# The beginning of a transformer block in two halves of the tokens: where column reads, the last transpose copies and the squares of the second half stand

## The chip, the cores and the metric

The kernel runs on one core of a Trainium2 chip. The metric is the device time of one launch in microseconds (us); lower is better. A core has TensorE (PE, with its weight loads PEld), VectorE (DVE), ScalarE (ACT), GpSimd (POOL), and SyncE (SP), which here issues most loads. Each engine works off its own instructions in the order in which they are written; between engines, an instruction waits for semaphores.

## What is computed

One layer of a diffusion transformer on 1024 latent tokens and 256 context tokens of width 1024. The parts that matter here come first in it:

```python
mod_x = (silu(c) @ w_mod + b_mod); mod_c = silu(c_ctx) @ w_mod + b_mod
sh1, sc1, ... = split(mod_x, 6);   csh1, csc1, ... = split(mod_c, 6)
h_x = rmsnorm(x,   g_pre_mix) * (1 + sc1)  + sh1
h_c = rmsnorm(ctx, g_pre_mix) * (1 + csc1) + csh1
u, q, k, v = split(h @ w_in)     # u: first 512 columns of w_in
```

Behind that stand a pooling mixer on u, neighbourhood attention with the context's keys, an output projection, and a squared-ReLU MLP, each with its norm and gate.

## The kernel before

The change touches the first 45 us alone. There the kernel normalises the latent tokens, turns them by 128 x 128 transposes on TensorE so that the width lies on the partitions, scales and shifts them with the modulation, and multiplies them with the first 512 columns of `w_in`.

**Tiles.** The tokens are eight tiles `x0` to `x7` of 128 rows. Tiles 0 to 3 are the first half (b = 0), tiles 4 to 7 the second (b = 1). The width is eight chunks k of 128. `xT[k]` holds chunk k of all tokens, turned. Each float32 operand is split in a high part (`fp32r`) and a low part (the rest), and a product is three passes: high x high, low weight x high operand, high weight x low operand. `wu0`, `wu1` ... are the weights for chunks 0 and 1, 2 and 3, ...; `wu0h` and `wu0l` are their parts; `hx0_1` is the operand of half 0 and chunk 1; `pu0_0` is the sum of output group 0 and half 0.

**The steps of a half.** `squared(n)` sums the squares of tile n on ScalarE (L154, 1024 columns, into `ms_x`). `rooted(n)` adds epsilon on VectorE (L159, `vt_x`) and raises to the power -1/2 on POOL (L163, `rt_x`). `normalised(n)` scales the tile on VectorE (L386). `turned` transposes one block on TensorE (L368) into a PSUM bank: `pxt0` to `pxt7` for the first half, one chunk each, and `pxb0` to `pxb2` for the second half, chunks 0 and 1, 2 and 3, 4 and 5. `put` and `kept_two` copy from there to `xT` (L373), on ScalarE or VectorE.

**The modulation.** For chunks 0 to 3, `chunk_sums(k, kh)` is 16 small matmuls (L402) of the modulation's weights with silu(c) and silu(c_ctx), in two halves kh of the inner width; a page of weights is loaded for each. `chunk_row` copies the row to SBUF (L406, `mrow`), `picked` turns it to columns on TensorE (L416), and `chunk_scale(k, pt, v)` makes scale `a1` (L431) and shift `s1` (L432) of chunk k on VectorE: v = 0 for the latent tokens, v = 1 for the context. The context's columns are used only much later, by `context`. `latent_high` makes the high part of an operand (L447 on ScalarE, L449 on VectorE), `latent_low` the low part (L453, then L454 on VectorE), `half_weight` the parts of half a weight page.

**Banks.** PSUM has six banks in the pool `ps1` and two lasting ones in `ps_t`. A name decides which:

```python
if name[:2] == "pm" or name in ("pxt5", "pxb2", "pxb3", "pxb4", "pct2", "pct3"):
    return lasting(name)                       # ps_t, 2 buffers
return ps1.tile([P, 512], F32, tag="mm", name=name)
```

So the lasting ones are taken in the order `pxt5`, `pm0_0` (chunk 0), `pm0_1` (chunk 1), `pxb2`, `pm1_0` (chunk 2), `pm1_1` (chunk 3), `pxb3` and so on. Each new tile takes over a buffer whose readers are done, and the first instruction that writes it waits for them. `picked` writes its columns into the same bank as the sums of its chunk, so that a bank of a chunk is read last by `chunk_scale`.

**What sets the order.** In this part the order on each engine is the order of the calls in the program: `in_order` keeps TensorE, ScalarE, VectorE, SyncE and POOL to it. All loads are issued by SyncE in the order: tiles 0 to 3, modulation pages and weights of chunks 0 and 1, tiles 4 to 7, pages and weights of chunks 2 and 3, pages of quarter 2, `wu2`, pages of quarter 3, `wu3`, the context.

Of the kernel before, what the change touches and what calls it, by code (L numbers as in the profile page):

```python
# [22 lines left out]
NT = SEQ // P  # L23
# [80 lines left out]
def hybrid_block(ctx, tc, x, ctx_in, w_mod, mod_pages, b_mod, gp1, gp2, w_in, pool_w, rpb, w_out, w1, w2, vectors,  # L104
# [14 lines left out]
    def sm(name, n, bufs=1):  # L119
        return small.tile([P, n], F32, tag=name.split("_")[0], name=name, bufs=bufs)  # L120

    def page(name, dt=F32):
        return act.tile([P, 1024], dt, tag="pg", name=name)
# [29 lines left out]
    def mean_square(junk, src, ms):  # L153
        nc.scalar.activation(junk, src, AF.Square, scale=D ** -0.5, accum_out=ms)  # L154

    def rsqrt_of(name, ms, more=None):
        v = sm(f"v{name}", 1, 4)
        if more is None:
            nc.vector.tensor_scalar_add(v, ms, EPS)  # L159
        else:  # L160
            nc.vector.scalar_tensor_tensor(v, ms, EPS, more, add, add)  # L161
        r = sm(f"r{name}", 1, 4)
        nc.gpsimd.tensor_tensor(r, v, nhalf, ALU.pow)  # L163
        return r
# [129 lines left out]
    with tc.tile_pool(name="ps1", bufs=6, space=PSUM) as ps1, tc.tile_pool(name="tmp1", bufs=3) as tmp:  # L294
# [75 lines left out]
        def put(copy, src, k, n):  # L370
            if xT[k] is None:
                xT[k] = page(f"xT{k}")
            copy(xT[k][:, n * P : n * P + src.shape[-1]], src)  # L373

        on_act, on_dve = nc.scalar.copy, nc.vector.tensor_copy
        means = {}

        def squared(n):
            means[n] = sm(f"ms_x{n}", 1, 4)
            mean_square(page(f"jkx{n}"), xn[n], means[n])  # L380

        def rooted(n):
            means[n] = rsqrt_of(f"t_x{n}", means[n])

        def normalised(n):
            nc.vector.tensor_scalar_mul(xn[n], xn[n], means[n])  # L386
# [28 lines left out]
        def picked(pt, mr, j):  # L415
            nc.tensor.matmul(pt[:, 4 * j : 4 * j + 4], mr[:, j * P : (j + 1) * P], pck, start=True, stop=True)  # L416
# [12 lines left out]
        def chunk_scale(k, pt, v):  # L429
            ks = slice(k, k + 1)  # L430
            nc.vector.scalar_tensor_tensor(a1[v][:, ks], pt[:, 2 + v : 3 + v], b_sc[:, ks], g1c[:, ks], add, mul)  # L431
            nc.vector.tensor_tensor(s1[v][:, ks], pt[:, v : v + 1], b_sh[:, ks], add)  # L432
# [10 lines left out]
        def latent_high(b, k, copy):  # L443
            h = hx[b][k] = page(f"hx{b}_{k}", F32R)
            src, scale, shift = xT[k][:, b * 512 : (b + 1) * 512], a1[0][:, k : k + 1], s1[0][:, k : k + 1]
            if copy is on_act:
                nc.scalar.activation(h[:, :512], src, AF.Identity, bias=shift, scale=scale)  # L447
            else:
                nc.vector.tensor_scalar(h[:, :512], src, scale, shift, mul, add)  # L449

        def latent_low(b, k):
            h, src = hx[b][k], xT[k][:, b * 512 : (b + 1) * 512]
            nc.vector.tensor_scalar(src, src, a1[0][:, k : k + 1], s1[0][:, k : k + 1], mul, add)  # L453
            nc.vector.tensor_tensor(h[:, 512:], src, h[:, :512].bitcast(F32), sub)  # L454
# [7 lines left out]
        def passes(b, js, k, n):  # L462
            if not pus[b]:
                pus[b] += [bank(f"pu{j}_{b}") for j in js]
            low, r = ((0, hx[b][k][:, :512]), (1, hx[b][k][:, :512]), (0, hx[b][k][:, 512:]))[n]
            for j in js:
                nc.tensor.matmul(pus[b][j], wk(wgt, k, low, j * P, P), r,  # L467
                                 start=(k == 0 and n == 0), stop=(k == KT - 1 and n == 2))

        def some_sums(b, js, k):  # L470
            for n in range(3):
                passes(b, js, k, n)
# [14 lines left out]
        def half_weight(q, i, part):  # L487
            cs = slice(i * 512, (i + 1) * 512)
            hi, lo = (t[:, cs] for t in wgt[q])
            part(raw_u[q][:, cs], hi, lo) if part is low_part else part(raw_u[q][:, cs], hi)  # L490

        pxt = [bank(f"pxt{k}") for k in range(5)] + [bank("pxt5"), bank("pxt6"), None]
        whole, pt = {}, {}

        def chunk_sums(k, kh):
            if kh == 0:
                whole[k] = bank(f"pm{k // 2}_{k % 2}")
            mod_sums(k // 2, whole[k], kh, k % 2)

        def chunk_row(k):  # L500
            pt[k] = whole[k][:, 384:388]
            return mod_kept(f"{k // 2}_{k % 2}", whole[k], P)

        def first_turned(n, ks):
            for k in ks:
                turned(pxt[k][:, n * P : (n + 1) * P], n, k)
# [21 lines left out]
        first_turned(3, range(4, KT - 1))  # L528
        put(on_act, pxt[0], 0, 0)
        half_weight(0, 0, lambda src, hi: nc.gpsimd.tensor_copy(hi, src))  # L530
        chunk_scale(0, pt[0], 0)
        put(on_dve, pxt[1], 1, 0)
        latent_high(0, 0, on_act)
        half_weight(0, 0, low_part)
# [3 lines left out]
        put(on_act, pxt[5], 5, 0)  # L538
        put(on_dve, pxt[4], 4, 0)
        put(on_dve, pxt[6], 6, 0)  # L540
        chunk_scale(0, pt[0], 1)
        chunk_sums(1, 0)
        passes(0, range(4), 0, 0)
        chunk_sums(1, 1)
# [3 lines left out]
        picked(pt[1], mr, 0)  # L548
        chunk_scale(1, pt[1], 0)
        latent_high(0, 1, on_dve)  # L550
        half_weight(0, 1, low_part)
        latent_low(0, 1)
        passes(0, range(4), 0, 2)
        pxt[7] = bank("pxt7")
        for n in range(4):
            first_turned(n, (7,))
        squared(4)
        put(on_act, pxt[7], 7, 0)
        for n in range(5, NT):
            squared(n)  # L560
        some_sums(0, range(4), 1)

        pxb = [bank(f"pxb{i}") for i in range(3)]
# [6 lines left out]
        def kept_two(copy, ks, n):  # L570
            for k in ks:
                put(copy, two(k), k, n)
# [4 lines left out]
                turned(ps[:, (n - 4) * P : (n - 3) * P], n, k)  # L577
            put(on_act, ps, k, 4)

        rooted(4)  # L580
        chunk_scale(1, pt[1], 1)
        rooted(5)
        normalised(4)
        rooted(6)
        normalised(5)
        rooted(7)
# [14 lines left out]
        kept_two(on_act, (2,), 6)  # L601
        mr = chunk_row(2)
        latent_high(1, 1, on_act)
        half_weight(1, 0, high_part)
        some_sums(1, range(2), 0)
        picked(pt[2], mr, 0)
        chunk_scale(2, pt[2], 0)
        latent_low(1, 1)
        latent_high(0, 2, on_act)
        half_weight(1, 0, low_part)  # L610
        latent_low(0, 2)
        kept_two(on_act, (4,), 6)
        kept_two(on_dve, (5,), 6)
        chunk_scale(2, pt[2], 1)
        for kh in range(2):
            chunk_sums(3, kh)
        mr = chunk_row(3)
# [858 lines left out]
    with tc.tile_pool(name="ps2", bufs=6, space=PSUM) as ps2:  # L1476
# [6 lines left out]
      with ExitStack() as tmp2:  # L1483
# [21 lines left out]
        def out_bank_sums(name, a, w):  # L1505
            ps = [bank(f"{name}_{t}") for t in range(4)]
            for t in range(4):
                out_sums(ps[t], a, w, t, True)
            return ps
# [32 lines left out]
        with tc.issue_after(projected[ET.DVE]), tc.issue_after(projected[ET.Activation]), in_order(ET.Activation, ET.DVE) as added:  # L1542
# [20 lines left out]
            v = out_bank_sums("pov", "S3", wt3)  # L1563
# [220 lines left out]
        def part(name):  # L1784
            return tmp.tile([P, 512], F32, tag="z", name=name, bufs=7)
# [263 lines left out]
        with tc.issue_after(first[ET.PE]), in_order(ET.PE, ET.Activation, ET.DVE, ET.SP):  # L2049
# [5 lines left out]
            def four(name):  # L2055
                return [bank(f"{name}_{t}") for t in range(4)]
# [78 lines left out]
            v, z = four("pyv"), four("pyz")  # L2135
# [68 lines left out]
```

## Time and profile before

| what | value |
|---|---|
| median of 3 runs | 1034.26 us (1032.35 to 1034.46) |
| profiled execution: time | 1033.65 us |
| profiled execution: span of the instructions | 1031.9 us |
| mean granted TensorE clock | 0.996 of full |
| TensorE busy, whole span | 1014.0 us (98%) |
| TensorE busy, 0 to 45 us | 35.66 us, granted clock 0.92 |
| TensorE busy, 45 to 200 us | 155.00 us, granted clock 1.00 |
| VectorE and ScalarE busy, 0 to 45 us | 22.59 and 23.47 us |
| DMA in the first 45 us | 373 GB/s, 97% of the 16 engines' time |

Times in the profile are counted from the first instruction. A row of the timeline gives start, duration, engine, line of the kernel, operation, what it writes and reads (without buffer numbers), a count where rows were merged, and in brackets how long the engine was idle before it and what ended that. An engine's name with a q is its sequencer, which issues DMAs. "issue" means that the profile shows nothing that the engine waited for. The granted clock is TensorE's clock as a share of full speed.

### The profile page before, as it was taken

The numbers are of one execution on the slowest core, as the hardware profiler recorded it, in microseconds if no ns is written. First come the engines' busy times: TensorE is split into PE (matmuls) and PEld (weight loads), VectorE is DVE, ScalarE is ACT, GpSimd is POOL, SyncE is SP. The second block draws the span as 40 slices with busy tenths as digits, with TensorE's granted clock in tenths as the row PEclk, the third lists the DMA queues.
The fourth block names the chain that finished last, engine by engine and source line by source line (L and its number), as shares of the span: only waits on it lengthen the run. The fifth ranks groups of instructions, "written<-read, shape, count | busy, mean of one in ns | idle before, by whom it ended". The sixth has DMA issues, their size and how long they took to land.

```text
span 1031.9 us, 16144 instructions
## 1 busy us (share of the span) xinstructions
PE 1014.0 (98%) x5962; PEld 839.8 (81%) x5962; DVE 747.8 (72%) x1164; ACT 544.2 (53%) x949; POOL 149.3 (14%) x231
## 2 busy tenths in 40 slices
PE   7899999999999999999999999999999999999997
PEld 6678888887898888888888888888888888888886
DVE  5578947877786687878998888855766666547576
ACT  5475155337888546776555544555543334334441
POOL 2011020047775312310000000000000000000002
PEclk9999999999999999999999999999999999999999
DMA  9769698814337965794786666636967766546555
GB/s 361 297 181 368 198 292 287 286 26 124 74 74 203 217 193 189 244 260 164 248 277 203 221 200 218 214 113 238 325 222 281 241 228 224 199 168 199 171 182 224
DMA packets 117023, 222.72 MB, mean 216 GB/s; under 512 B 9488, under 2 KB 46992, under 8 KB 116944
## 3 DMA queue, kind: packets, MB, share of 16 engines
q1 hardware_dynamic: 90448, 171.14, 49.2%
q0 software_dynamic: 9360, 19.58, 9.4%
q10 hardware_dynamic: 17136, 30.97, 8.0%
q8 instruction: 47, 0.77, 0.3%
q14 instruction: 32, 0.26, 0.1%
HBM read 168.16 MB, written 52.45 MB: 214 GB/s over the span
## 4 chain that ended last, share of the span: by engine, by line
PE 95%; POOL 1%; ACT 1%; issue 1%; DVE 1%; DMA 0%; POOLq 0%; DVEq 0%; ACTq 0%
PE pu L467 4%; PE pa L1247 3%; PE phz L221 3%; PE phv L221 3%; PE phx L221 3%; PE pyx L221 3%; PE phx L223 3%; PE phz L223 3%; PE phv L223 3%; PE pyx L222 3%; PE pyx L223 3%; PE pyv L222 3%; PE pyv L221 3%; PE pyz L222 3%; PE pyz L221 3%; PE phx L222 3%
## 5 line engine op out<-in xcount | busy, mean ns | idle before, releaser
L1193 ACT ACTIVATE sp<-sp,nm 128x640 f32<-128x640 f32 (+1 forms) x64 | 51.5, 804 | 9.6 <-DVE ri L1197 4.9
L1182 DVE CUSTOM_DVE_ANT_0 sp<-S,tab 128x640 f32<-128x640 f32 (+1 forms) x56 | 44.5, 795 | 14.1 <-PE pz L1213 9.6
L1789 ACT ACTIVATE c<-c 128x512 f32<-128x512 f32 x48 | 30.3, 631 | 46.0 <-DVE c L1909 26.6
L169 ACT CAST wpS<-S 128x512 fp32r<-128x512 f32 x64 | 38.8, 616 | 28.1 <-DVE S L1762 11.3
L221 PE MATMUL phx<-thB,wpA 128*128 128x512 f32 x128 | 50.2, 392 | 0.0
L223 PE MATMUL phx<-thB,wpA 128*128 128x512 f32 x128 | 49.8, 389 | 0.0
L222 PE MATMUL phx<-tlB,wpA 128*128 128x512 f32 x128 | 49.8, 389 | 0.0
L175 DVE TENSOR_TENSOR wpS<-S,wpS 128x512 fp32r<-128x512 f32 x64 | 43.5, 687 | 8.5 <-ACT wpS L169 8.3
L163 POOL TENSOR_TENSOR ry<-vy,nhalf 128x1 f32<-128x1 f32 x8 | 5.9, 739 | 281.5 <-DVE vy L161 281.5
L1790 ACT ACTIVATE c<-c 128x512 f32<-128x512 f32 x48 | 30.3, 630 | 14.5 <-DVE sa L1872 13.7
L221 PEld LDWEIGHTS phx<-thB,wpA 128*128 128x128 f32 x128 | 24.0, 188 | 5.5 <-ACT s L1840 0.5
L223 PEld LDWEIGHTS phx<-thB,wpA 128*128 128x128 f32 x128 | 24.0, 188 | 5.1
L222 PEld LDWEIGHTS phx<-tlB,wpA 128*128 128x128 f32 x128 | 24.1, 188 | 4.8
L1232 DVE COPY pt<-T 128x512 f32<-128x512 f32 x32 | 22.0, 686 | 5.8 <-PE T L1213 5.8
L1247 PE MATMUL pa<-pt,v 128*64 128x128 f32 x352 | 25.9, 279 | 0.2
L221 PE MATMUL phz<-thB,wpS 128*128 128x512 f32 x64 | 25.0, 391 | 0.0
L221 PE MATMUL phv<-thT,wpA 128*128 128x512 f32 x64 | 25.0, 391 | 0.0
L223 PE MATMUL phv<-thT,wpA 128*128 128x512 f32 x64 | 24.9, 389 | 0.0
L223 PE MATMUL phz<-thB,wpS 128*128 128x512 f32 x64 | 24.9, 389 | 0.0
L222 PE MATMUL phz<-tlB,wpS 128*128 128x512 f32 x64 | 24.9, 389 | 0.0
L221 PE MATMUL phy<-thT,wpS 128*128 128x512 f32 x64 | 24.9, 389 | 0.0
L222 PE MATMUL phy<-tlT,wpS 128*128 128x512 f32 x64 | 24.9, 389 | 0.0
(1139 smaller groups left out, 3440.1 us busy)
## 6 DMA issues: line engine op xcount, KB each, us to landing
b<-in_w SPq DMA_DIRECT2D x64, 512.0 KB, 4.1
hrS<-hdS SPq DMA_DIRECT2D x32, 512.0 KB, 5.1
hrA<-hdA SPq DMA_DIRECT2D x24, 512.0 KB, 5.4
wm<-in_mod_pages SPq DMA_DIRECT2D x16, 512.0 KB, 9.7
wa_0w<-in_w SPq DMA_DIRECT2D x16, 512.0 KB, 5.1
wa_1w<-in_w SPq DMA_DIRECT2D x16, 512.0 KB, 4.3
hdA<-c ACTq DMA_DIRECT2D x32, 256.0 KB, 2.6
hdS<-sa ACTq DMA_DIRECT2D x32, 256.0 KB, 2.3
```

The source lines that it names most:

```text
L169: nc.scalar.copy(hi, src)
L175: nc.vector.tensor_tensor(lo, src, hi.bitcast(F32), sub)
L221: nc.tensor.matmul(ps, ahi, bhi, start=first, stop=False, skip_group_check=more)
L222: nc.tensor.matmul(ps, ahi, blo, start=False, stop=False, skip_group_check=more)
L223: nc.tensor.matmul(ps, alo, bhi, start=False, stop=last, skip_group_check=more)
L467: nc.tensor.matmul(pus[b][j], wk(wgt, k, low, j * P, P), r, start=(k == 0 and n == 0), stop=(k == KT - 1 and n == 2))
L1182: nc.vector.tensor_tensor_reduce(out=to, in0=s, in1=bt, scale=1.0, scalar=BIG, op0=add, op1=ALU.min, accum_out=nm)
L1193: nc.scalar.activation(sp, sp, AF.Exp, bias=least[i, e], scale=-1.0, accum_out=sums[i][:, e : e + 1])
L1232: copy(turns[i].rearrange("p e i t -> p (e i) t")[:, :, h * HD : (h + 1) * HD], turned[i][h].rearrange("p (a t) -> p a t", a=8))
L1247: nc.tensor.matmul(pa[e * HD : (e + 1) * HD, cols], v[:, f : f + HD], turns[i][:, e, c] if c < 4 else fifths[i][:, :, (e + 1) * HD : (e + ...
L1789: nc.scalar.activation(r, src, AF.Relu)
L1790: nc.scalar.activation(r, r, AF.Square)
```

## The change

Only the order of calls changes; no instruction is added or taken away, and TensorE's own order stays as it was.

```diff
@@ first half, behind the turning of tiles 0 to 3
         half_weight(0, 0, lambda src, hi: nc.gpsimd.tensor_copy(hi, src))
-        chunk_scale(0, pt[0], 0)
+        for v in range(2):
+            chunk_scale(0, pt[0], v)
         put(on_dve, pxt[1], 1, 0)
...
         put(on_dve, pxt[6], 6, 0)
-        chunk_scale(0, pt[0], 1)
         chunk_sums(1, 0)
...
         latent_high(0, 1, on_dve)
+        squared(4)
+        rooted(4)
         half_weight(0, 1, low_part)
-        latent_low(0, 1)
         passes(0, range(4), 0, 2)
         pxt[7] = bank("pxt7")
         for n in range(4):
             first_turned(n, (7,))
-        squared(4)
+        squared(5)
         put(on_act, pxt[7], 7, 0)
-        for n in range(5, NT):
+        for n in (6, 7):
             squared(n)
+        latent_low(0, 1)
         some_sums(0, range(4), 1)
@@ second half, roots and scaling of tiles 4 to 7
-        rooted(4)
-        chunk_scale(1, pt[1], 1)
         rooted(5)
         normalised(4)
+        chunk_scale(1, pt[1], 1)
         rooted(6)
@@ second half, first products
         latent_high(1, 1, on_act)
+        kept_two(on_act, (4,), 6)
+        kept_two(on_dve, (5,), 6)
         half_weight(1, 0, high_part)
         some_sums(1, range(2), 0)
         picked(pt[2], mr, 0)
-        chunk_scale(2, pt[2], 0)
+        for v in range(2):
+            chunk_scale(2, pt[2], v)
         latent_low(1, 1)
         latent_high(0, 2, on_act)
         half_weight(1, 0, low_part)
         latent_low(0, 2)
-        kept_two(on_act, (4,), 6)
-        kept_two(on_dve, (5,), 6)
-        chunk_scale(2, pt[2], 1)
         for kh in range(2):
             chunk_sums(3, kh)
```

What this does to the queues, at three places. Names carry a number of their buffer at the end, which differs between the two kernels where a page is taken earlier or later.

**VectorE and TensorE, chunk 0.** `a10`, `s10` are scale and shift for the latent tokens, `a11`, `s11` for the context. VectorE before:

```order
L432 TENSOR_TENSOR s10_170<-pm0_0_183,cols_93 128x1
L373 COPY xT1_302<-pxt1_177 128x512
L175 TENSOR_TENSOR wu0l_173<-wu0w_103,wu0h_172 128x512
L453 TENSOR_SCALAR xT0_297<-xT0_297,a10_168,s10_170 128x512
L454 TENSOR_TENSOR hx0_0_304<-xT0_297,hx0_0_304 128x512
L373 COPY xT4_315<-pxt4_180 128x512
L373 COPY xT6_317<-pxt6_182 128x512
L431 TENSOR_SCALAR a11_169<-pm0_0_183,cols_93 128x1
L432 TENSOR_TENSOR s11_171<-pm0_0_183,cols_93 128x1
```

VectorE in the changed kernel:

```order
L432 TENSOR_TENSOR s10_170<-pm0_0_183,cols_93 128x1
L431 TENSOR_SCALAR a11_169<-pm0_0_183,cols_93 128x1
L432 TENSOR_TENSOR s11_171<-pm0_0_183,cols_93 128x1
L373 COPY xT1_304<-pxt1_177 128x512
L175 TENSOR_TENSOR wu0l_173<-wu0w_103,wu0h_172 128x512
```

And TensorE at the sums of chunk 1 (`pm0_1`) and the first products, in brackets the engines and loads (DMAHW) whose semaphores it waits for:

```order
-L402 MATMUL pm0_1_321<-wm0_1_0_109,sT_159 32x128 [waits DMAHW0_49,Activation_49]
+L402 MATMUL pm0_1_321<-wm0_1_0_109,sT_159 32x128 [waits DMAHW0_49,DVE_49,PE_49]
 L402 MATMUL pm0_1_321<-wm0_1_0_109,sT_159 32x128 x7
-L467 MATMUL pu0_0_330<-hx0_0_304,wu0h_172 128x512 [waits Pool_49]
-L467 MATMUL pu1_0_331<-hx0_0_304,wu0h_172 128x512 [waits DVE_49]
-L467 MATMUL pu2_0_332<-hx0_0_304,wu0h_172 128x512
-L467 MATMUL pu3_0_333<-hx0_0_304,wu0h_172 128x512
+L467 MATMUL pu0_0_330<-hx0_0_306,wu0h_172 128x512 [waits Activation_49,Pool_49]
+L467 MATMUL pu1_0_331<-hx0_0_306,wu0h_172 128x512 [waits DVE_49]
+L467 MATMUL pu2_0_332<-hx0_0_306,wu0h_172 128x512 [waits Activation_49]
+L467 MATMUL pu3_0_333<-hx0_0_306,wu0h_172 128x512 [waits Activation_49]
```

The context's columns of chunk 0 are read ahead of three copies and a split. With that `pm0_1` takes over the bank of `pm0_0`, where it took that of `pxt5`, and the sums wait for VectorE and no longer for ScalarE. ScalarE's copies are now waited for by the products.

**ScalarE, the squares of tiles 4 to 7** (`jkx4` is the throw-away output of tile 4's square). Before:

```order
L406 COPY mrow0_1_346<-pm0_1_321 128x128
L169 COPY wu0h_172<-wu0w_103 128x512
L154 ACTIVATE jkx4_371,ms_x4_370<-x4_114 128x1024
L373 COPY xT7_373<-pxt7_365 128x512
L154 ACTIVATE jkx5_376,ms_x5_375<-x5_116 128x1024
L154 ACTIVATE jkx6_379,ms_x6_378<-x6_118 128x1024
L154 ACTIVATE jkx7_382,ms_x7_381<-x7_120 128x1024
```

In the changed kernel:

```order
L169 COPY wu0h_172<-wu0w_103 128x512
L154 ACTIVATE jkx4_359,ms_x4_358<-x4_114 128x1024
L154 ACTIVATE jkx5_376,ms_x5_375<-x5_116 128x1024
L373 COPY xT7_378<-pxt7_370 128x512
L154 ACTIVATE jkx6_381,ms_x6_380<-x6_118 128x1024
```

The square of tile 5 now stands ahead of the copy of chunk 7 instead of behind it. On VectorE the small operation for tile 4's root (L159) moves from behind the low part of `hx0_1` to ahead of the second half of `wu0l`, and tile 4's scaling ahead of chunk 1's context columns.

**VectorE, the last copy of the second half's chunk 5** (`pxb2`), around the columns of chunk 2 (`pm1_0`). Before:

```order
L454 TENSOR_TENSOR hx1_0_469<-xT0_297,hx1_0_469 128x512
L431 TENSOR_SCALAR a10_168<-pm1_0_432,cols_93 128x1
L432 TENSOR_TENSOR s10_170<-pm1_0_432,cols_93 128x1
L453 TENSOR_SCALAR xT1_302<-xT1_302,a10_168,s10_170 128x512
L454 TENSOR_TENSOR hx1_1_478<-xT1_302,hx1_1_478 128x512
L175 TENSOR_TENSOR wu1l_175<-wu1w_122,wu1h_174 128x512
L453 TENSOR_SCALAR xT2_309<-xT2_309,a10_168,s10_170 128x512
L454 TENSOR_TENSOR hx0_2_494<-xT2_309,hx0_2_494 128x512
L373 COPY xT5_313<-pxb2_398 128x256
L431 TENSOR_SCALAR a11_169<-pm1_0_432,cols_93 128x1
L432 TENSOR_TENSOR s11_171<-pm1_0_432,cols_93 128x1
```

In the changed kernel:

```order
L454 TENSOR_TENSOR hx1_0_469<-xT0_297,hx1_0_469 128x512
L373 COPY xT5_315<-pxb2_402 128x256
L431 TENSOR_SCALAR a10_168<-pm1_0_432,cols_93 128x1
L432 TENSOR_TENSOR s10_170<-pm1_0_432,cols_93 128x1
L431 TENSOR_SCALAR a11_169<-pm1_0_432,cols_93 128x1
L432 TENSOR_TENSOR s11_171<-pm1_0_432,cols_93 128x1
L453 TENSOR_SCALAR xT1_304<-xT1_304,a10_168,s10_170 128x512
L454 TENSOR_TENSOR hx1_1_478<-xT1_304,hx1_1_478 128x512
```

The copy moves ahead of six larger operations and of the columns of chunk 2. On ScalarE the copy of chunk 4 from the same bank moves ahead of the cast of `wu1h` and of the activation of `hx0_2`. The sums of chunk 3 (`pm1_1`) take over this bank.

## The prediction

> **What bounds the kernel now.** First the page's busy times: TensorE (PE) works 98% of the span, so the end moves only if TensorE works less or waits less. Then the waits of TensorE, and a table of stages.
>
> ```profile
> PE 1014.0 (98%) x5962; PEld 839.8 (81%) x5962; DVE 747.8 (72%) x1164; ACT 544.2 (53%) x949; POOL 149.3 (14%) x231
> PE pm L402 <- issue: 3.7, 1, 3.7
> PE pm L402 <- ACT xT L373: 2.4, 1, 2.4
> 40.00:200.00 160.00, 160.00 (x780) 130.91 (x779) 118.01 (x192) 75.14 (x120) 14.96 (x17) 1.00 0.84 260
> ```
>
> The last row (stretch, its length, busy time of PE, PEld, DVE, ACT, POOL, then the granted clock) says that from 40 to 200 us TensorE never stops, at full clock. All that the change touches lies before 45 us, and there are two long waits of TensorE there, both before sums of the modulation (L402). What is won there is kept if nothing behind it waits for something that does not move along.
>
> The same table in steps of 3.41 us shows a second loss: the clock.
>
> ```profile
> 12.27:15.68 3.41, 1.42 (x21) 0.95 (x9) 2.30 (x6) 2.76 (x6) 0.61 (x1) 1.00 1.04 418
> 15.68:19.10 3.42, 3.05 (x24) 1.80 (x26) 1.73 (x5) 0.31 (x1) 0.00 (x0) 0.50 1.03 416
> 25.92:29.34 3.42, 3.32 (x45) 2.55 (x47) 2.19 (x6) 2.27 (x9) 1.27 (x2) 1.00 1.04 410
> 29.34:32.75 3.41, 2.57 (x24) 1.48 (x16) 2.34 (x7) 2.57 (x6) 0.00 (x0) 1.00 1.03 401
> 32.75:36.16 3.41, 0.23 (x9) 0.26 (x13) 3.20 (x8) 0.88 (x2) 0.00 (x0) 1.00 1.04 409
> 36.16:39.58 3.42, 3.42 (x37) 2.65 (x29) 0.00 (x0) 1.81 (x4) 0.00 (x0) 0.50 1.03 399
> ```
>
> After a stretch with 1.42 or 0.23 us of TensorE work the next one is granted half the clock; after 2.57 us or more it stays at 1.00.
>
> **Part 1, both columns of chunk 0 at once: the first wait.** Rows of the timeline: start, duration, engine, line, operation, count, in brackets the idle time before.
>
> ```profile
> 11.89 0.38 PEld L402 LDWEIGHTS pm<-wm,sT 128*32 128x32 f32 x16 [0.16 <-issue]
> 12.47 0.42 PEld L368 LDWEIGHTS pxt<-ident,x 128*128 128x128 f32 x4 [0.20 <-issue]
> 13.48 0.15 DVE L432 TENSOR_TENSOR s<-pm,cols 128x1 f32<-128x1 f32 x1
> 13.73 0.81 ACT L447 ACTIVATE hx<-xT,s,a 128x512 fp32r<-128x512 f32 x1 [0.31 <-DVE s L432]
> 14.45 1.54 ACT L373 COPY xT<-pxt 128x512 f32<-128x512 f32 x3
> 16.05 1.08 PE L402 MATMUL pm<-wm,sT 128*32 128x128 f32 x16 [2.35 <-ACT xT L373]
> 4.81 0.33 SPq L322 DMA_DIRECT2D wm<-in_mod_pages  x1
> wm<-in_mod_pages SPq DMA_DIRECT2D x1, 512.0 KB, 9.0
> 19.06 0.65 PE L402 MATMUL pm<-wm,sT 128*32 128x128 f32 x16
> ```
>
> The sums of chunk 1 need one of two lasting banks. Before, the context's columns of chunk 0 are read late, so the bank that comes free first is that of pxt5, whose copy is the third of ScalarE's, done at 15.99. Now VectorE reads those columns right behind 13.48: two more operations of that length, done by about 13.9, and the wait is for them. The page of these sums lands at 4.81 + 9.0 = 13.8. So the sums start at 13.9, not 16.05, and last 0.58 to the next start (11.89 to 12.47). The four products behind them then meet their own waits: the operand is ready at 13.73 + 0.81 = 14.54, and the fourth needs the bank that ScalarE's second copy frees, at about 15.5. It starts at 15.6, the second sums one product later (about 0.25, by the products at full clock below), at 15.9 instead of 19.06: TensorE is 3.2 us ahead. The price: VectorE's copy and splits behind 13.48 are some 0.2 us later; none is wanted before 16.4, so this costs nothing.
>
> **Part 2, squares sooner: what keeps the 3.2.** TensorE would reach the turning of tiles 4 to 7 at 25.34 - 3.2 = 22.1. It needs their norms: square (ScalarE), root (POOL), scaling (VectorE).
>
> ```profile
> 23.86 1.37 POOL L163 TENSOR_TENSOR rt_x<-vt_x,nhalf 128x1 f32<-128x1 f32 x2 [10.60 <-DVE vt_x L159]
> 11.03 0.33 SPq L316 DMA_DIRECT2D x<-in_x  x1
> x<-in_x SPq DMA_DIRECT2D x1, 512.0 KB, 10.9
> 25.34 1.60 PE L368 MATMUL pxb<-ident,x 128*128 128x128 f32 x12
> 25.03 1.06 ACT L154 ACTIVATE jkx<-x 128x1024 f32<-128x1024 f32 x1
> 30.04 0.85 PE L467 MATMUL pu<-hx,wu0h 128*128 128x512 f32 x2 [0.30 <-ACT hx L447]
> ```
>
> Before, the square of tile 7 starts at 25.03, the last of three in a row that begin only behind a copy which waits for TensorE. With the sums 3.2 earlier and the square of tile 5 ahead of that copy, ScalarE would be ready for tile 7 before it is there: it lands at 11.03 + 10.9 = 21.9. So its square starts at 21.9, 3.1 earlier, and the chain behind it (root, scaling, six transposes, copies, first operand) is as long as before: the first product of the second half comes at 26.9 instead of 30.04. **First term: 3.1 us.** A root may be up to 0.4 shorter or longer, by the two in the POOL row. The small operation that now stands ahead of wu0l's second half on VectorE waits for ScalarE's square of tile 4; if that were late, wu0l and the two splits of chunk 1 would be held, and TensorE's second pass. The second half of wu0l is wanted about 1 us after chunk 1's first pass starts; that covers it.
>
> **Part 3, last copies ahead: the second wait.**
>
> ```profile
> 30.39 0.83 ACT L447 ACTIVATE hx<-xT,s,a 128x512 fp32r<-128x512 f32 x1
> 30.60 0.69 DVE L454 TENSOR_TENSOR hx<-xT,hx 128x512 fp32r<-128x512 f32 x1
> 31.92 0.28 PE L416 MATMUL pm<-cols,mrow 128*128 128x4 f32 x2
> 33.01 0.69 DVE L454 TENSOR_TENSOR hx<-xT,hx 128x512 fp32r<-128x512 f32 x1
> 33.28 0.35 ACT L373 COPY xT<-pxb 128x256 f32<-128x256 f32 x1
> 35.41 0.42 DVE L373 COPY xT<-pxb 128x256 f32<-128x256 f32 x1
> 35.93 1.76 PE L402 MATMUL pm<-wm,sT 128*32 128x128 f32 x32 [3.72 <-issue]
> ```
>
> The sums of chunk 3 take the lasting bank of pxb2, which two copies empty: ScalarE's at 33.28 and VectorE's at 35.41, done at 35.83, 0.1 before TensorE goes on. The profile names only "issue", but that copy is the one thing that ends there. Now ScalarE's stands behind the activation of 30.39 (30.39 + 0.83 = 31.2, done by 31.6), VectorE's behind it and behind 30.60 + 0.69 = 31.29, done by 31.6 + 0.42 = 32.0. TensorE's two picks end at 31.92 + 0.28 = 32.20, so it goes straight on. **Second term: 3.7 us**, the idle time. Late next is VectorE's low part of hx1_1: it ended at 33.01 + 0.69 = 33.7, and the context's two column operations, now ahead of it, push it to about 33.9 on this clock. Its pass comes at 32.2 + 1.16 (sums) + 0.98 (two passes, both from the next paragraph) = 34.3, 0.4 later. That cover is thin: each tenth beyond it would be lost.
>
> **The clock.** With 3.7 us of idle gone, the half clock from 36.16 goes too.
>
> ```profile
> 37.62 1.22 PE L467 MATMUL pu<-hx,wu0h 128*128 128x512 f32 x2
> 40.15 1.17 PE L467 MATMUL pu<-hx,wu1h 128*128 128x512 f32 x4
> 43.34 0.71 PE L467 MATMUL pu<-hx,wu1h 128*128 128x512 f32 x2
> 44.81 0.60 PE L368 MATMUL pxb<-ident,x 128*128 128x128 f32 x4
> ```
>
> The 32 sums took 37.62 - 35.93 = 1.69; at full clock 2 x 0.58 = 1.16: **0.5 us**. Six products and two picks took 40.15 - 37.62 = 2.53; at full clock six products take 44.81 - 43.34 = 1.47, and the picks 0.1: **0.9 us**. The half clock at 15.68 lies inside the first term, since what bounds there is the landing of tile 7.
> [...]
>
> **Behind that.** The other moved rows (chunk 2's columns, the order of casts) only change places while TensorE is busy. Loads do not move along, as the DMA engines are full until 44 us. The one that is split first behind the sum's last term is wu2:
>
> ```profile
> 25.16 0.38 SPq L201 DMA_DIRECT2D wu2w<-in_w_in  x1
> wu2w<-in_w_in SPq DMA_DIRECT2D x1, 512.0 KB, 9.7
> 47.61 1.06 ACT L171 ACTIVATE wu2h<-wu2w 128x1024 fp32r<-128x1024 f32 x1
> ```
>
> It lands at 25.16 + 9.7 = 34.9 and would be wanted at 47.61 - 8.2 = 39.4, with 4.5 us to spare. The pages of quarter 2 stand ahead of it in the same queue and are here sooner.
>
> **Sum.** 3.1 + 3.7 + 0.5 + 0.9 = 8.2 us. The profiled execution took 1033.65 us, so 1025.45. The median of the runs shown is 1034.26, 0.6 above it; the mean of the four executions is 1033.7, and from that I forecast 1025.5.
>
> **Rivals.**
> A. The first term is lost: the norms of tiles 4 to 7 (four roots in a row on POOL, each between a small operation and a scaling on VectorE) bind in the old place. For it: the turning of tile 4 at 25.34 already came behind a scaling. Against: that chain starts with the square, and this is freed. Leaves 5.1: 1028.6.
> B. The second half's turning is granted half the clock. In the changed kernel that part has short waits for tiles 5, 6 and 7, and its work is mostly transposes. Against: 25.92:29.34 holds the turning of tiles 5 to 7 and little else (sixteen sums take 0.65 us), and the next row is at 1.00. The price is at most half of a stretch, 1.7 us: 1027.2. [...]
> C. The second wait stays, on another reader of the bank, with its half clock; only 3.1 us are won: 1030.6. Against: 35.83 fits the copy alone.
> D. Slower. Between 75 and 100 us the weights of the next stage come in; TensorE shows no wait there, so how near it is cannot be read. If these loads came at the old time, TensorE would wait there for the 8.2 us that it is ahead, longer than a whole stretch of 3.41, and run the next one at half clock: 1.7 us slower than now, 1035.4. It decides where the lead passes the slack of those loads. Against: they are issued when VectorE and ScalarE release buffers, which move along.
>
> **How the numbers follow.** Forecast 0.70, A 0.14, B 0.06, C 0.05, D 0.05. Two per mille, 2.1 us, is about the spread of the runs before (1032.35 to 1034.46) and about what a measurement can tell from no change. Forecast, A, B and C are all beyond it on the fast side, D beyond only just on the slow side: faster 0.93, same 0.03, slower 0.04. The range goes down to 1023.6 (the lowest run is 1.3 below the mean, a shorter root gives 0.4, rounded down) and up to 1029.0, past A by 0.4; C and D are left out.
>
> **What would show it.** Right: the waits of 2.35 and 3.72 us gone from TensorE, no stretch at 0.50 after the start, the square of tile 7 starting at about 21.9 right at its landing, the first product of the second half near 26.9, the products of chunk 2 (40.15 before) near 32.0, and the same lead at 200 us. Wrong: a new wait over 1 us of TensorE before 45 us, a stretch at 0.50 between 20 and 40, or a lead that shrinks between 45 and 200 us.

## The result and the profile after

The changed kernel takes 1025.52 us (median of 6 runs, 1024.85 to 1026.2), the kernel before in the same comparison 1034.36 (6 runs, 1032.35 to 1036.17). The ratio is 0.9918, with a 95% interval of 0.9904 to 0.9931: 8.5 us faster (the medians lie 8.8 apart, since the six runs before scatter over 3.8 us). The profiled execution took 1025.65 us with a span of 1023.9, against 1033.65 and 1031.9.

First the page's busy times, TensorE's waits in the first 70 us, and the stages of the changed kernel (stretch, length, busy time of PE, PEld, DVE, ACT, POOL, granted clock):

```profile
PE 1012.5 (99%) x5962; PEld 838.5 (82%) x5962; DVE 747.8 (73%) x1164; ACT 544.8 (53%) x949; POOL 149.8 (15%) x231
PE pm L365 <- POOL ident masks.py:199: 1.6, 1, 1.6
PE pxt L368 <- DVE x L386: 0.4, 1, 0.4
PE pm L402 <- DMA wm<-in_mod_pages: 0.3, 1, 0.3
PE pu L467 <- ACT hx L447: 0.3, 1, 0.3
0.00:45.00 45.00, 42.22 (x347) 32.42 (x348) 27.36 (x77) 28.48 (x54) 8.74 (x16) 1.00 0.98 377
45.00:200.00 155.00, 155.00 (x730) 127.64 (x729) 119.16 (x185) 72.46 (x117) 14.97 (x17) 1.00 0.86 268
```

The waits of 2.4 and 3.7 us are gone. In the first 45 us TensorE is busy 42.22 us instead of 35.66, at a granted clock of 1.00 instead of 0.92, and from 45 to 200 us it never stops, as before (155.00 of 155 us). Most of what is left idle lies ahead of the first product: the largest wait, 1.6, is for the identity at the very start.

The timeline of the changed kernel, at the rows that answer to those of the prediction:

```profile
13.95 0.64 PE L402 MATMUL pm<-wm,sT 128*32 128x128 f32 x16 [0.30 <-DMA wm<-in_mod_pages]
15.94 0.64 PE L402 MATMUL pm<-wm,sT 128*32 128x128 f32 x16
22.51 1.76 PE L368 MATMUL pxb<-ident,x 128*128 128x128 f32 x12
22.16 1.04 ACT L154 ACTIVATE jkx<-x 128x1024 f32<-128x1024 f32 x1
27.37 0.84 PE L467 MATMUL pu<-hx,wu0h 128*128 128x512 f32 x2 [0.30 <-ACT hx L447]
28.44 0.37 ACT L373 COPY xT<-pxb 128x256 f32<-128x256 f32 x1
28.84 0.42 DVE L373 COPY xT<-pxb 128x256 f32<-128x256 f32 x1 [0.22 <-ACT xT L373]
29.25 0.28 PE L416 MATMUL pm<-cols,mrow 128*128 128x4 f32 x2
29.46 1.08 PE L402 MATMUL pm<-wm,sT 128*32 128x128 f32 x32
30.47 0.73 PE L467 MATMUL pu<-hx,wu0h 128*128 128x512 f32 x2
32.11 1.17 PE L467 MATMUL pu<-hx,wu1h 128*128 128x512 f32 x4
```

The sums of chunk 1 start at 13.95 and no longer at 16.05, and what they wait for is now a load. VectorE's copy out of the bank of `pxb2` ends at 28.84 + 0.42 = 29.26, while TensorE is still in the picks of 29.25, so the sums of chunk 3 follow at 29.46 without a wait. Two leads can be read off: the first product of the second half stands at 27.37 instead of 30.04, 2.67 earlier, and the products of chunk 2 at 32.11 instead of 40.15, 8.04 earlier. The last instruction ends 8.0 earlier (span 1023.9 against 1031.9).

### The profile page after: what moved, and what is told of

Read it like the earlier page. It is cut to its first block, busy times and chain, and to the rows that moved or that the text cites. A ratio compares the mean times of both kernels' runs of the same rounds, so it can differ in the third digit from the quotient of the medians.

```text
span 1023.9 us, 16144 instructions
## 1 busy us (share of the span) xinstructions
PE 1012.5 (99%) x5962; PEld 838.5 (82%) x5962; DVE 747.8 (73%) x1164; ACT 544.8 (53%) x949; POOL 149.8 (15%) x231
## 4 chain that ended last, share of the span: by engine, by line
PE 95%; DMA 2%; POOL 1%; ACT 1%; issue 0%; DVE 0%; SPq 0%; DVEq 0%; POOLq 0%; ACTq 0%
PE pu L467 4%; PE pa L1248 4%; PE phz L221 3%; PE phv L221 3%; PE phx L221 3%; PE pyx L221 3%; PE pyx L223 3%; PE phx L223 3%; PE pyv L222 3%; PE pyz L222 3%; PE phz L223 3%; PE pyx L222 3%; PE phv L223 3%; PE pyv L223 3%; PE pyz L223 3%; PE phx L222 3%
## 5 line engine op out<-in xcount | busy, mean ns | idle before, releaser
L221 PE MATMUL phv<-thT,wpA 128*128 128x512 f32 x64 | 25.0, 391 | 0.0
L222 PE MATMUL phv<-tlT,wpA 128*128 128x512 f32 x64 | 24.9, 389 | 0.0
```

The costliest lines, as they stand in the source:

```text
L221: nc.tensor.matmul(ps, ahi, bhi, start=first, stop=False, skip_group_check=more)
L222: nc.tensor.matmul(ps, ahi, blo, start=False, stop=False, skip_group_check=more)
```

## The experiments

The theory has three parts: the bank that the sums of chunk 1 take over (first wait), the copies out of `pxb2` (second wait), and the clock, which was at 0.50 behind the stretches with 1.42 and 0.23 us of TensorE work. The rivals for each were another reader of the bank, a chain of norms or loads that binds in the old place, and another cause of the half clock. The first four kernels split the change; the kernel before beside them took 1034.14 us (median). Runs e5 to e8 stood beside runs of 1033.77.

**e1: the columns of chunk 0 alone.**

```diff
+        for v in range(2):
+            chunk_scale(0, pt[0], v)
-        chunk_scale(0, pt[0], 0)
...
-        chunk_scale(0, pt[0], 1)
```

> The kernel before with one edit: both columns of chunk 0 are read at once. Theory (the bank): the 2.35 us wait of TensorE at the first sums of chunk 1 shrinks to 0.3, the first product of the second half comes 2.2 to 3.1 us earlier than 30.04, the wait of 3.7 us at the sums of chunk 3 stays with its half clock, and the time falls by as much as the first product, 2.2 to 3.1 us (ratio 0.997 to 0.998). Rival (the squares bind in their old place): the first product of the second half moves by less than 1 us and the time by less than 1 us. Rival (the lead is eaten by the second wait): the second wait grows to 6 us and the time stays.

Measured: 1031.51 us, ratio 0.9974 (0.9964 to 0.9983). Its timeline:

```profile
13.99 0.64 PE L402 MATMUL pm<-wm,sT 128*32 128x128 f32 x16 [0.26 <-DVE s L432]
27.22 0.85 PE L467 MATMUL pu<-hx,wu0h 128*128 128x512 f32 x2 [0.30 <-ACT hx L447]
33.10 1.94 PE L402 MATMUL pm<-wm,sT 128*32 128x128 f32 x32 [3.73 <-issue]
```

The first wait goes, the first product comes 2.82 earlier than in the kernel before, and the second wait stays whole. So the wait of 2.35 us hung on the bank; e7, below, frees the old bank sooner and shortens the wait too.

**e2: the last two copies alone.**

```diff
+        kept_two(on_act, (4,), 6)
+        kept_two(on_dve, (5,), 6)
         half_weight(1, 0, high_part)
...
-        kept_two(on_act, (4,), 6)
-        kept_two(on_dve, (5,), 6)
```

> The kernel before with one edit: the two copies out of pxb2 for tiles 6 and 7 stand ahead of the cast of wu1h; chunk 2's columns stay where they were. Theory (the copy on VectorE frees the bank, and the idle stretch costs the clock): the wait of 3.7 us goes, no half clock behind it, 5.1 us faster (ratio 0.995). Rival (the idle time alone): 3.7 us. Rival (another reader of the bank, chunk 2's context columns among them): the wait stays and the time is the same within 1 us.

Measured: 1028.43 us, ratio 0.994 (0.9928 to 0.9952). Its timeline:

```profile
16.15 0.64 PE L402 MATMUL pm<-wm,sT 128*32 128x128 f32 x16 [2.35 <-ACT xT L373]
32.55 1.08 PE L402 MATMUL pm<-wm,sT 128*32 128x128 f32 x32
33.56 0.73 PE L467 MATMUL pu<-hx,wu0h 128*128 128x512 f32 x2
35.20 1.17 PE L467 MATMUL pu<-hx,wu1h 128*128 128x512 f32 x4
```

Now the first wait stays and the second goes, though the profile of before named "issue" for it. The 32 sums take 33.56 - 32.55 = 1.01 to the next start, at full clock (1.00 from 20.09 to 47.39). VectorE's copy moves ahead of five larger operations here, and not of six as was said above: before, they stand between 32.44 and 35.41. By medians e1 wins 2.6 and e2 5.7, a little more than the 5.1 expected; between the profiled executions it is 5.1 (1033.65 to 1028.55). Together e1 and e2 win 8.3, against the 8.6 that e4, below, wins beside the same runs with both edits and chunk 2's columns. Those columns were not run alone; what is left for them is within the noise.

**e3: the squares alone, and e4: everything but the squares.** e3 puts the change's lines on `squared`, `rooted` and the low part of chunk 1 into the kernel before; e4 takes the same lines out of the changed kernel:

```diff
-        squared(4)
-        rooted(4)
         half_weight(0, 1, low_part)
+        latent_low(0, 1)
...
-        squared(5)
+        squared(4)
         put(on_act, pxt[7], 7, 0)
-        for n in (6, 7):
+        for n in range(5, NT):
             squared(n)
-        latent_low(0, 1)
...
+        rooted(4)
+        chunk_scale(1, pt[1], 1)
         rooted(5)
         normalised(4)
-        chunk_scale(1, pt[1], 1)
```

> The kernel before with the edit of the squares alone: tile 4's square and root operation ahead of the low part of wu0's second half, tile 5's square ahead of chunk 7's copy, chunk 1's low part behind. Theory: ScalarE's idle 0.85 us ahead of that copy is used, the square of tile 7 starts 0.8 us earlier, the first product of the second half 0.5 to 0.8 us earlier, and the time falls by 0.5 to 0.8 us; both long waits stay. Rival (VectorE is held at the root operation): the low parts come later, TensorE waits in its second pass, and the time is the same or up to 1 us longer.

> The changed kernel with the edit of the squares undone: chunk 0's and chunk 2's columns at once and the copies ahead stay. Theory (with the first wait gone, the landing of tile 7 and ScalarE's row of squares bind, with little left for their order): first product of the second half within 0.6 us of the changed kernel's 27.37, time within 0.6 us of 1025.5. Rival (the order of the squares carries the first term): first product at 28.5 or later, time 1 us or more longer.

Measured: e3 1034.15 us, ratio 0.9996 (0.9988 to 1.0004); e4 1025.54 us, ratio 0.9915 (0.9902 to 0.9928), the time of the changed kernel. The last product ahead of the turning of tiles 4 to 7, that turning, and the first product behind it, in e3; then the square of tile 7 and the first product in e4:

```profile
24.34 1.08 PE L467 MATMUL pu<-hx,wu0h 128*128 128x512 f32 x4
25.26 1.52 PE L368 MATMUL pxb<-ident,x 128*128 128x128 f32 x12
29.88 0.85 PE L467 MATMUL pu<-hx,wu0h 128*128 128x512 f32 x2 [0.30 <-ACT hx L447]
22.04 1.05 ACT L154 ACTIVATE jkx<-x 128x1024 f32<-128x1024 f32 x1
27.21 0.85 PE L467 MATMUL pu<-hx,wu0h 128*128 128x512 f32 x2 [0.30 <-ACT hx L447]
```

Both waits stay in e3. Its turning starts at 25.26, where TensorE comes free, so the earlier squares bring only 0.16 us of first product (29.88 against 30.04), less than the 0.5 to 0.8 expected. Part of that is this execution: its first half-clock stretch lies at 16.80 to 20.22 instead of 15.68 to 19.10, and TensorE reaches that last product 0.23 later than in the kernel before. By the interval of its times e3 could still be up to 1.2 us faster. e4 is the sharper test: its four runs (1025.39 to 1025.87) lie within those of the changed kernel, and its first product stands at 27.21, no later than there. So the third part of the change is worth nothing that these runs can tell, alone or with the others.

**e5 and e6: the idle time of the second wait filled.** In the kernel before, TensorE is given work without use, ahead of the sums of chunk 3:

```diff
         chunk_scale(2, pt[2], 0)
+        for _ in range(28):
+            nc.tensor.transpose(whole[2][:, 128:256], ident, ident)
         latent_low(1, 1)
```

e6 has 14 matmuls of the identity with itself in that place.

> The kernel before with 28 spare transposes of the identity on TensorE, written into an unused part of chunk 2's bank, right ahead of the sums of chunk 3: they fill most of the 3.7 us wait there and change no other order. Their output is used by nothing. Theory (the idle time is what halves the clock behind it): the sums of chunk 3 still start near 35.9 us, because the bank of pxb2 is still emptied by VectorE's copy, but no stretch at 0.50 follows; 32 sums take 1.0 to 1.2 us and not 1.7, six products 1.5 and not 2.5, and the kernel is 1.2 to 2.2 us faster than before although it does more. Rival 1 (the half clock has another cause, the mix of work for one): the stretch at 0.50 stays and the time is that of before within 0.5 us. Rival 2 (transposes do not count as busy): the stretch stays here, and is gone in the run with plain matmuls.

> The same with 14 plain 128 x 128 float32 matmuls in place of the 28 transposes. Theory: as there, no stretch at 0.50 behind the wait, 1.2 to 2.2 us faster than before. Rival 1: as before within 0.5 us. Rival 2 (transposes do not count): faster here by 1.2 to 2.2 us, and not with transposes.

Measured: e5 1032.78 us, ratio 0.9988 (0.9979 to 0.9997); e6 1032.94 us, 0.9992 (0.9983 to 1.0001). Timeline and table of stretches of e5:

```profile
32.73 3.28 PE L609 MATMUL pm<-ident 128*128 128x128 f32 x28 [0.38 <-DVE s L432]
36.08 1.08 PE L402 MATMUL pm<-wm,sT 128*32 128x128 f32 x32
37.09 0.74 PE L467 MATMUL pu<-hx,wu0h 128*128 128x512 f32 x2
38.74 1.17 PE L467 MATMUL pu<-hx,wu1h 128*128 128x512 f32 x4
32.98:36.39 3.41, 3.34 (x40) 3.13 (x42) 3.21 (x8) 0.80 (x2) 0.00 (x0) 1.00 1.04 409
36.39:39.80 3.41, 3.41 (x42) 2.75 (x34) 0.88 (x4) 2.12 (x4) 0.00 (x0) 1.00 1.03 401
```

The sums still start late, at 36.08, but at full clock: 1.01 us instead of 1.69, and the six products and picks behind them 38.74 - 37.09 = 1.65 instead of 2.53. The products of chunk 2 come 1.41 earlier, in both kernels. So the idle time is what halved the clock here (0.23 us of work in that stretch of the kernel before, 3.34 in e5), and it costs about what the prediction took for it. The 3.34 us of the stretch 32.98 to 36.39 are almost all transposes, and the next is at 1.00. In e6, with matmuls, the stretches from 30.91 to 37.73 hold 3.03 and 3.41 us, and the ones behind them are at 1.00 too. So the second rival falls. By medians the gain is 1.0 and 0.8 us, below the 1.2 expected, and e6's interval includes no gain at all: what shows the clock's part is the table, more than the times. Of the 1.41 in e5's profile 0.3 are lost again later in the span, and where was not followed up.

**e7: the bank of `pxt5` freed first.** The columns of chunk 0 stay as they were; ScalarE copies `pxt5` ahead of two others:

```diff
+        put(on_act, pxt[5], 5, 0)
         put(on_act, pxt[2], 2, 0)
         put(on_act, pxt[3], 3, 0)
-        put(on_act, pxt[5], 5, 0)
```

> The kernel before with one change on ScalarE: the copy of pxt5 is the first of its three copies there instead of the third. The columns of chunk 0 stay in two parts. Bank theory: the sums of chunk 1 wait for that copy alone and start near 15.1 instead of 16.05, a wait of about 1.4 us; the products behind them then wait for ScalarE's later copies, so that the second sums start near 16.5 to 17.5 instead of 19.06; with more of the stretch filled, the half clock behind it may go. 1 to 2.7 us faster, as in the run with both columns of chunk 0 at once (2.7 us there). Rival (the sums wait for the columns or for the landing of their page): the wait stays at 2.3 us and the time that of before.

Measured: 1031.68 us, ratio 0.9983 (0.9974 to 0.9992). Its timeline, then the stretches around its two waits:

```profile
15.08 0.64 PE L402 MATMUL pm<-wm,sT 128*32 128x128 f32 x16 [1.38 <-ACT xT L373]
16.79 0.64 PE L402 MATMUL pm<-wm,sT 128*32 128x128 f32 x16
27.76 0.85 PE L467 MATMUL pu<-hx,wu0h 128*128 128x512 f32 x2 [0.30 <-ACT hx L447]
12.33:15.74 3.41, 2.03 (x35) 1.41 (x26) 2.35 (x6) 2.81 (x6) 0.61 (x1) 1.00 1.04 419
15.74:19.16 3.42, 3.42 (x29) 2.50 (x30) 2.09 (x8) 1.93 (x5) 0.00 (x0) 1.00 1.02 411
29.39:32.80 3.41, 0.53 (x4) 0.38 (x2) 2.77 (x7) 1.13 (x3) 0.00 (x0) 1.00 1.03 401
32.80:36.21 3.41, 2.56 (x34) 2.11 (x35) 0.94 (x4) 0.57 (x2) 0.00 (x0) 0.50 1.03 408
36.21:39.63 3.42, 3.42 (x11) 2.75 (x10) 0.93 (x4) 1.54 (x3) 0.00 (x0) 0.50 1.04 401
```

One copy put first takes 0.97 us off the wait. The stretch now holds 2.03 us of work instead of 1.42, and the half clock behind it is gone. The first product comes at 27.76, 2.28 earlier: the shortened wait won more than its own length. In this profiled execution only 1.05 of the 2.28 are left at the end (1032.6 against 1033.65); here two stretches at 0.50 follow the second wait instead of one.

**e8: tile 7 one page later.** In the changed kernel the first modulation page of chunk 2 is loaded ahead of tile 7:

```diff
-        xn += token_tiles(1)
+        xn += [token_tile(f"x{n}", x[n * P : (n + 1) * P, :]) for n in range(4, 7)]
+        wm[1][0][0] = mod_load(1, 0, 0)
+        xn.append(token_tile("x7", x[7 * P : 8 * P, :]))
...
```

> The changed kernel with the load of chunk 2's first modulation page moved ahead of the load of tile 7, so that tile 7 lands one page, about 1.28 us, later. Theory (in the changed kernel the beginning of the second half is set by the landing of tile 7 and the chain behind it): the square of tile 7 starts near 23.4, the first product of the second half near 28.6 instead of 27.37, and the kernel takes 1.0 to 1.3 us longer than the changed kernel, 1026.5 to 1026.9. Rival (the chain of roots and scalings of the tiles before binds): first product within 0.3 us of 27.37 and the time that of the changed kernel.

Measured: 1026.67 us (5 runs, 1026.22 to 1027.07), ratio to before 0.9935 (0.9922 to 0.9947), 1.15 above the changed kernel by medians and 1.02 between the profiled executions. Its timeline (three lines were added above, so L405 is L402, and so on):

```profile
22.01 1.66 PE L371 MATMUL pxb<-ident,x 128*128 128x128 f32 x12
23.30 1.06 ACT L154 ACTIVATE jkx<-x 128x1024 f32<-128x1024 f32 x1 [1.43 <-DMA x<-in_x]
24.48 0.15 DVE L159 TENSOR_SCALAR vt_x<-ms_x 128x1 f32<-128x1 f32 x1 [1.74 <-ACT jkx L154]
25.70 1.73 PE L371 MATMUL pxb<-ident,x 128*128 128x128 f32 x12 [1.46 <-DVE xT L376]
28.31 0.85 PE L470 MATMUL pu<-hx,wu0h 128*128 128x512 f32 x2 [0.30 <-ACT hx L450]
```

ScalarE waits 1.43 us for the tile, and its square starts 1.14 later than in the changed kernel. VectorE waits 1.74 us for that square: the small operation for tile 7's root stands ahead of tile 6's scaling, so both tiles are late, and TensorE waits 1.46 us for a copy that stands behind that scaling on VectorE. The first product is 0.94 later, less than the 1.2 expected; the part below on the first term says where the other 0.2 lie. So a later tile 7 holds the second half up. It does not follow that a sooner one would help: in the changed kernel ScalarE comes free for the square (22.16) just as the tile lands (22.1). Apart from the start, the changed kernel has about 1 us of TensorE waits left in 45 us.

## Why the prediction was right

**Sum.** 8.2 us were predicted for the profiled execution, 8.0 came (1033.65 to 1025.65), and the lead of 8.04 at the products of chunk 2 is kept to the end. Two terms were mis-sized, in opposite directions: 3.1 came as 2.67, and 5.1 as 5.37. That the median of 1025.52 falls on the forecast of 1025.5 is in part luck, since these errors partly cancel.

**First term, 3.1 forecast, 2.67 in the profile and 2.82 in e1.** The bank and the landing of its page were read rightly (sums at 13.95 for 13.9, second sums at 15.94 for 15.9). Two steps failed by a little: that ScalarE would be ready for tile 7 "before it is there", and that the chain behind the square "is as long as before". The loads of tiles 7 and 4 in the changed kernel (both took the 11.1 us of the third row), and what hangs on them:

```profile
11.00 0.33 SPq L316 DMA_DIRECT2D x<-in_x  x1
7.15 0.33 SPq L316 DMA_DIRECT2D x<-in_x  x1
x<-in_x SPq DMA_DIRECT2D x1, 512.0 KB, 11.1
18.30 1.06 ACT L154 ACTIVATE jkx<-x 128x1024 f32<-128x1024 f32 x1 [0.87 <-DMA x<-in_x]
19.49 0.15 DVE L159 TENSOR_SCALAR vt_x<-ms_x 128x1 f32<-128x1 f32 x1 [0.76 <-ACT jkx L154]
20.30 1.20 PE L467 MATMUL pu<-hx,wu0l 128*128 128x512 f32 x4
24.62 0.74 DVE L386 TENSOR_SCALAR x<-x,rt_x 128x1024 f32<-128x1024 f32 x1
25.40 0.86 PEld L368 LDWEIGHTS pxb<-ident,x 128*128 128x128 f32 x8 [0.20 <-ACT xT L373]
```

Tile 7 lands at 11.0 + 11.1 = 22.1 for 21.9 and is squared at 22.16, 2.87 earlier than before. ScalarE had no idle time ahead of that square: until then it was at the square of tile 6, so the landing and ScalarE bind together. From that square to tile 7's scaling it is 24.62 - 22.16 = 2.46 us, as before (27.49 - 25.03); from there to the first product 27.37 - 24.62 = 2.75 us, for 2.55 before. In e1, e4 and e8 that part is 2.55 or 2.56 too; only the changed kernel has the extra 0.2, and the next paragraph says where they come from.

**The cover that was named did not hold.** Tile 4 lands at 7.15 + 11.1 = 18.25, so its square starts at 18.30, and the small root operation, now ahead of `wu0l`'s second half, held VectorE for 0.76 us. `wu0l` was ready at 19.56 + 0.68 = 20.24, and the pass that needs it starts at 20.30. The turning of tiles 4 to 7 then begins at 22.51; in e8, where tile 4 came sooner, at 22.01, which is the 22.1 of the prediction. The hold goes on behind that: the operation for tile 5's root, which stands behind the held work on VectorE, comes at 21.34, though that tile's square was done at 20.74. Tile 5 is scaled at 22.59 (22.22 in e1), ScalarE's five copies end at 25.36 (24.98 in e1), and TensorE's last eight transposes wait for them, by the last row above. In e1, e4 and e8 only six are left when tile 7 is ready. These are the 0.2 us. No run takes the hold out alone; this is read from the traces. That 0.2 and not 0.5 reached the end is luck of the loads, since tile 7 came later still, and not the cover of "about 1 us" that the prediction counted on.

**The squares.** The prediction gave them a part in keeping the lead ("the square of tile 5 ahead of that copy"). e4 has the lead without them: with the first wait gone, ScalarE's old order already reaches tile 7 at 22.04. The lead was kept, but not by the squares.

**Second term and clock, 5.1 forecast, 5.37 in the profile.** From the first product of the second half to the products of chunk 2 it was 40.15 - 30.04 = 10.11 us and is 32.11 - 27.37 = 4.74. Of the 5.37, the sums give 1.69 - 1.01 = 0.68 where 0.5 was taken, since two rows of 16 sums side by side were priced at 0.58 each and 32 in one run take 1.01; the products and picks give 2.53 - 1.64 = 0.89, as forecast; the rest, 3.80, is the wait of 3.72 and 0.08 of small differences. The low part of hx1_1, named as late next, ended in time, and TensorE has no gap there.

**The rivals.** A (norms bind in the old place): the chain moved with the square, in e1 even without the edit of the squares. B (half the clock for the second turning): the changed kernel is granted 1.00 in all of the first 45 us, and e5's stretch of transposes is followed by one at 1.00. C (another reader of the bank): in e2 the wait goes with the copies alone. D (loads between 75 and 100 us): TensorE is busy for all of 45 to 200 us, and the lead does not shrink.

**The median.** One trace does not show how the clock varies between executions; the runs do, in the last section. Against the fastest run of before in the same comparison (1032.35) the median of the change is 6.8 us faster, and 8.5 on average.

## What to carry to other kernels

Where a pool hands out few lasting buffers in the order of the names, look for the reader that empties each one last, and put the short reads ahead of the long work on its engine: two small column reads and two copies, moved apart from each other, won 2.6 and 5.7 us here by themselves, while squares that were merely started sooner won nothing that could be told. Price an idle stretch of TensorE with the clock behind it (3.41 us at 0.50 behind each of the two waits here), and a shortened one too. And a small operation that waits for a load does not belong ahead of work that TensorE is waiting for, unless the load is known to be in: here it held VectorE for 0.76 us.

## What the runs showed of the hardware

**The clock followed the work in the stretch before.** The stretches at 0.50 in the kernel before last 3.41 us each (15.68 to 19.10 and 36.16 to 39.58) and start 20.48 us, six such lengths, apart. In all ten profiles, from about 5 to 45 us, a stretch of 3.41 us at full clock with 0 to 1.58 us of TensorE work was followed by one at 0.50, and one with 1.96 us or more by one at 1.00. It took more to come back from half clock: 2.56 us of work at 0.50 left the next stretch of e7 at 0.50 too, and 3.05 us or more brought the full clock back. e3 had two half stretches in a row:

```profile
30.46:33.87 3.41, 1.58 (x7) 0.92 (x6) 2.43 (x6) 2.17 (x4) 0.00 (x0) 1.00 1.04 398
33.87:37.28 3.41, 1.51 (x31) 1.51 (x32) 1.96 (x6) 0.00 (x0) 0.00 (x0) 0.50 1.02 408
37.28:40.70 3.42, 3.42 (x17) 2.49 (x9) 0.00 (x0) 2.11 (x4) 0.00 (x0) 0.50 1.04 399
```

So the same wait of 3.73 us cost one half-clock stretch in e1 and two in e3 and e7: it depended on where the stretches fell. They are not tied to the kernel's work: the first one at 0.50 begins at 15.68 in the kernel before, 16.67 in e2 and 16.80 in e3, while the wait at that place ends at 16.05, 16.15 and 16.10. The 27 runs of the kernel before beside e5 to e8 show the same as a spread of the time against the mean granted clock of the span:

| runs | time | granted clock |
|---|---|---|
| 9 | 1032.31 to 1032.57 us | 0.997 to 0.998 |
| 12 | 1033.58 to 1034.02 us | 0.995 to 0.996 |
| 3 | 1034.38 to 1034.75 us | 0.994 |
| 3 | 1035.98 to 1036.24 us | 0.993 |

The changed kernel has 0.998 or 0.999 in every run, and a spread of 1.35 us instead of 3.9. So an execution of the kernel before may lose less than the profiled one (1033.65 us at 0.996), as nine of the 27 do, or more, as the last six do.

**A pause in the loads.** The 512 KB loads of tiles 4 to 7 are issued 1.26 to 1.30 us apart and mostly land so too, but one of them lands about 1 us late, and not always the same: tile 6 in the kernel before (10.9 us from issue to landing, where tiles 4 and 5 took 9.9; it lands 2.3 behind tile 5), tile 4 in the changed kernel (11.1 us; it lands 2.5 behind the load before it, where the kernel before has 1.3). In e8 too, ScalarE waits for tile 6 until 20.72, 2.2 behind the square of tile 5. What causes it stays open. It is the reason why the hold on VectorE shows in the changed kernel, where tile 4's square starts at 18.30, and not in e8, where it starts at 17.44.
